# An eighth ring slot, spaced loads and a new visit order in a transformer block's down projection, with one score pipeline in its attention stage

## The chip, the cores and the metric

The kernel runs on one core of a Trainium2 chip. The metric is the device time of one execution in microseconds, taken as the median of three runs. Engines are named as in the profile: PE is TensorE, DVE is VectorE, ACT is ScalarE, POOL is GpSimd and SP is SyncE. PEclk is the clock that was granted to PE, as a share of full speed.

## The reference

One block: a normed input projection, a state-space mixer (SSD) beside a sparse attention (NSA), an output projection, and a gated feed-forward. There are 512 tokens of width 2048, the feed-forward is 5632 wide, and everything is in fp32.

```python
u = rmsnorm(h, attn_norm_w[l])
z, xbc, dt_raw, q, kc, vc, ks, vs, kw, vw, gate_raw = jnp.split(u @ w_in[l], split_at, axis=-1)
y_ssd = ssd_mixer(z, xbc, dt_raw, conv_w[l], conv_b[l], dt_bias[l], a_log[l], d_skip[l], ssd_norm_w[l])
y_att = nsa_mixer(q, kc, vc, ks, vs, kw, vw, gate_raw, cmp_w1_k[l], cmp_w2_k[l], cmp_w1_v[l], cmp_w2_v[l], cmp_pe_k[l], cmp_pe_v[l], cos, sin)
mixed = jnp.concatenate([y_ssd.astype(h.dtype), y_att.astype(h.dtype)], axis=-1)
h = h + mixed @ w_out[l]
v = rmsnorm(h, ffn_norm_w[l])
h = h + (jax.nn.silu(v @ w_gate[l]) * (v @ w_up[l])) @ w_down[l]
```

The SSD mixer's output y*silu(z) is normed over 1024 channels ahead of the output projection. The attention has 16 heads in 4 groups that share keys and values. It sums three gated branches: over keys and values compressed by a small MLP, over selected blocks (all 8 blocks of 64 tokens are selected here, so this is causal attention), and over a window of 512. A last rmsnorm closes the block.

## The kernel before, in words

**Arithmetic.** Activations lie with features on the partitions and the 512 tokens along the free axis. Every fp32 operand is split into a high part, rounded to the matmul format fp32r, and a low remainder, and every product is three matmuls: hi x hi, hi x lo, lo x hi. ACT makes the high part (`a_hi`, L118), DVE the low part (`lo`, L121), of weights too. `mul` is L124 and `add` L127.

**Order.** The program is written as coroutines. `Sched` (L67) holds tasks; `sch.tick()` after each step of a matmul group moves every task on by one, `yield n` lets n ticks pass, and `wait` holds a task until flags are set. This gives an order in which instructions are written. Outside `tc.manual_schedule()` the framework's scheduler may reorder them; inside it each engine runs them as written. Each engine works its own list strictly in order.

**Projection units.** `run_unit` (L222) computes 128 output features from 16 (w_in) or 8 (w_out) blocks of 128 weights (L241 to L243, 128x512). Weights arrive as `wraw` and become `whi` and `wlo`. The result lies in one of the PSUM banks ps_t, ps_s, ps_g, two each; a task then evacuates it and sets a flag ("evac", n) at its end, and unit n waits for the flag of unit n-2. Units run in the order `order`: dt and gates, the SSD's B, C and X, keys and values to be compressed, Z; then, for each group, values, keys and two of queries.

**Attention stage.** Before the first values unit, `pre_att` (L1010) ticks until the compressing MLP is done and swaps pools. From there on all units but the last run in `manual_schedule` (L1790). `attention` (L829) takes the groups in turn: it waits for a group's keys, values and queries, does the softmax over the compressed keys, and then sends 32 items (4 heads, 2 branches, 4 blocks of 128 rows) through 15 steps, a new item every second step: score (PE), mask and maximum (DVE, L893), exp (ACT), normalizing, transposes (PE, L926), high and low parts (`pth`, `ptl`), value matmuls (PE, L949). At a group's end the pipeline runs empty. `ev_os` (L1071) evacuates w_out's units over the SSD half of the features; the first makes the statistics of the SSD norm (`rms_stats`, "r2") and puts them into rrow. `acc2` gathers the squares of h1, the sum of x and this half. `pre_oa` drains all tasks; its `stat_s` makes the statistics of h1 (L292, L302), and OA (L1252 on, 128x512) adds the attention half of w_out.

**Gate, up and down.** These use Strassen-Winograd products: 7 products (M1 to M7) of 128x256 in place of 8, on weight quadrants 11, 12, 21, 22 and their sums S1, S3 (`quad`). `run_step` first calls `prep(s.i + 2)`, so high and low parts are made two steps ahead, in zones of R and E. For each of the 22 units u of 256 features, `g_forms` (L1457) makes the 7 forms of the gated product, high and low, in staging rows ST of the tile A (rows 44 to 72), and stores them as g_d[u], from ACT's DMA queue (L1476).

The down projection has 8 output blocks j. `VISITS` (L23) lists which j takes how many of the 22 G's at a time; sums stay in the H tiles, which `load_h` fetches. `feed` (L1541) loads a G into one of `GRING` = 7 slots, from ACT's queue, two steps after the slot's last reader (`done`). The slots lie in tiles that the gate and up projections use until their end (`start_ff`, V0, VV and T, 8 rows each, of which a G takes 7). `down_before` (L1695) loads the next H at product 1 of each visit, and opens the pool A2, rows 70 to 75 of A, for weight sums.

Of the kernel before, what the change touches and what calls it, by code (L numbers as in the profile page):

```python
# [11 lines left out]
ALU = mybir.AluOpType  # L12
# [10 lines left out]
VISITS = [(0, 3), (1, 4), (2, 5), (3, 5), (4, 5), (5, 5), (6, 5), (7, 4), (0, 4), (7, 4), (4, 5), (1, 5), (6, 5), (2, 5),  # L23
          (5, 5), (3, 6), (0, 4), (7, 4), (6, 5), (4, 6), (1, 5), (5, 6), (2, 6), (3, 5), (0, 5), (7, 4), (1, 4), (6, 4),
          (7, 6), (6, 3), (3, 6), (5, 6), (1, 4), (2, 6), (4, 6), (0, 6)]
GRING = 7
# [21 lines left out]
V_SLOT = [0, 1, 4, 5, 3, 2, 6]  # L48
# [60 lines left out]
def body(ctx, tc, xT, w_in, w_out, w_gate, w_up, w_down, w1k, w1v, cols, rows, kst, out):  # L109
# [46 lines left out]
    g_d = dram.tile([NP, 4, 128, 896], F32, name="g_d")  # L156

# [63 lines left out]

    def run_unit(u):  # L222
# [8 lines left out]
        p = p[:, 0:u.cols[1] - u.cols[0]]  # L231
        for i, k0, n in u.sub:
# [89 lines left out]
    def ev_dtg(p):  # L322
# [3 lines left out]
        mul(dve, t, p[0:64, :], rrow[0:64, :])  # L326
        yield 2
# [46 lines left out]
    def conv(t, p):  # L374
# [4 lines left out]
        mul(dve, xp[:, 3:515], p, rrow)  # L379
        y = sp.tile([128, 512], F32, tag="c", name="cv", bufs=3)  # L380
# [179 lines left out]
    def ev_z(t):  # L560
        def ev(p):
            yield from sch.wait("r1", ("y", t // 4))
            g, j = divmod(t, 4)
            if g == 0:
                sp = pools["ssd"][1]
                zs = sp.tile([128, 512], F32, tag="zs", name="zs", bufs=2)
                mul(dve, zs, p, rrow)
                act.activation(zs, zs, AF.Silu)
# [4 lines left out]
            else:  # L573
# [6 lines left out]
                mul(dve, zs, p, rrow)  # L580
                yield 1
# [16 lines left out]
    def ev_kc(g):  # L598
        def ev(p):
# [5 lines left out]
            for n, b in (("kc2", 0), ("vc2", 64)):  # L605
                for par in range(2):
                    mul(dve, R[n][par * 64:par * 64 + 64, g, :], p[b:b + 64, par::2], rrow[b:b + 64, par::2])
            if g == 3:
                sch.flags.add("kc")
# [91 lines left out]
    def ev_vs(g):  # L701
        def ev(p):
# [4 lines left out]
            mul(dve, t, p, rrow)  # L707
            yield 2
# [39 lines left out]
    def ev_ks(g):  # L748
        def ev(p):
# [4 lines left out]
            mul(dve, t, p, rrow)  # L754
            yield 1
# [32 lines left out]
    def ev_q(g, j):  # L788
        def ev(p):
# [4 lines left out]
            mul(dve, t, p, rrow)  # L794
            yield 1
# [32 lines left out]

    def attention():  # L829
        yield from sch.wait("att", "cmp")  # L830
        ap = pools["att"][1]
        vpad = ap.tile([128, 4, 128], F32R, name="vpad")
# [3 lines left out]
        for g in range(4):  # L836
            yield from sch.wait(("k", g), ("v", g), ("q", g, 0), ("q", g, 1))
            kh, kl = R["k", g]
            v = R["v", g]

            sc = R["sc", g]
            sm = ap.tile([128, 3, 4, 4], F32, tag="sm", name="sm", bufs=1)
            dve.tensor_reduce(sm[:, 0], sc, AX.X, ALU.max)
            dve.tensor_scalar(sm[:, 0], sm[:, 0], -1e20, None, op0=ALU.max)
# [1044 lines left out]
```

## Time and profile before

| What | Value |
|---|---|
| three runs | 2313.32, 2312.17, 2308.17 us |
| median | 2312.17 us |
| the profiled execution (span; the profile gives no other time for it) | 2311.7 us |
| units of w_in, attention and w_out end | at 818 us |
| OA begins | at 827 us |
| first matmul of the down projection | at 1800 us |
| PE busy | 2196.5 us, 95% |
| DVE, ACT, POOL busy | 1809.7, 1091.2, 422.2 us |
| bytes moved by DMA | 417.34 MB, mean 181 GB/s |

In the lists of waits, a row names the engine, the tile it writes and its line, then the releaser with its tile and line, and the total, the number and the longest of the waits in us. In the time lines a row has the start, the length, the engine, the line and the operation, and in brackets the idle time before it with its releaser. A window's row gives for each engine the busy time and, behind x, the number of instructions.

### The profile page before, as it was taken

To read this page: it belongs to the slowest core of one execution; us is meant where nothing else is said; L and a number is where in the kernel's file an instruction comes from. 1 tells how busy PE (TensorE), PEld (TensorE's weight loads), DVE (VectorE), ACT (ScalarE), POOL (GpSimd) and SP (SyncE) were. 2 spreads that over 40 slices of the span, in tenths; PEclk is the share of its full clock that TensorE was granted. 3 is DMA by queue.
4 is the path that set the end of the run, shared out by engine and by line. 5 is a ranking of instruction groups with operands and counts; after the bars stand their busy time and mean duration, and the time that the engine had idled before them with its cause. 6 is when DMAs were issued, how large, how long until landed. Compare 5 with 4: busy or idle time off the path is not lost. (4 is left out here: it accounts for less than half of the span.)

```text
span 2311.7 us, 39742 instructions
## 1 busy us (share of the span) xinstructions
PE 2196.5 (95%) x15376; PEld 2039.8 (88%) x15376; DVE 1809.7 (78%) x2921; ACT 1091.2 (47%) x1768; POOL 422.2 (18%) x435
## 2 busy tenths in 40 slices
PE   7999988989989989999999999999999698989997
PEld 5888877878878878999999999999999698989997
DVE  7799754768788857888888888888888697878786
ACT  4554433757676634544444444444444243333353
POOL 1011214132232134100000000000101121212122
PEclk9999989999999999999999999999999899999998
DMA  5222432221233366787878787887878857677776
GB/s 176 89 74 74 133 110 87 73 72 63 76 101 125 105 198 180 207 233 219 242 217 243 221 249 226 245 227 231 233 219 250 323 170 264 186 254 233 259 162 171
DMA packets 151469, 417.34 MB, mean 181 GB/s; under 512 B 16320, under 2 KB 21968, under 8 KB 151280
## 3 DMA queue, kind: packets, MB, share of 16 engines
q1 hardware_dynamic: 99264, 250.99, 31.5%
q0 software_dynamic: 25456, 76.78, 17.3%
q10 hardware_dynamic: 26560, 87.04, 10.5%
q8 instruction: 120, 1.97, 0.3%
q14 instruction: 69, 0.57, 0.1%
HBM read 353.67 MB, written 57.15 MB: 178 GB/s over the span
## 5 line engine op out<-in xcount | busy, mean ns | idle before, releaser
L118 ACT ACTIVATE R<-Z 128x1024 fp32r<-128x1024 f32 (+4 forms) x488 | 441.5, 922 | 573.0 <-DVE Z L127 320.6
L121 DVE TENSOR_TENSOR R<-Z,R 128x1024 fp32r<-128x1024 f32 (+4 forms) x381 | 392.3, 1035 | 28.5 <-ACT R L118 19.7
L241 PE MATMUL ps_g<-u,whi 128*128 128x512 f32 x720 | 301.1, 418 | 9.5 <-ACT whi L118 9.5
L242 PE MATMUL ps_g<-u,whi 128*128 128x512 f32 x720 | 284.3, 395 | 0.0
L243 PE MATMUL ps_g<-u,wlo 128*128 128x512 f32 x720 | 284.3, 397 | 0.0
L1252 PE MATMUL ps_g<-u,R 128*128 128x256 f32 (+1 forms) x834 | 250.5, 300 | 0.7 <-ACT R L118 0.7
L1253 PE MATMUL ps_g<-u,R 128*128 128x256 f32 (+1 forms) x834 | 249.7, 299 | 0.0
L1254 PE MATMUL ps_g<-u,R 128*128 128x256 f32 (+1 forms) x674 | 200.5, 298 | 0.1
L1252 PE MATMUL ps_t<-u,R 128*128 128x256 f32 x688 | 194.0, 282 | 0.0
L1253 PE MATMUL ps_t<-u,R 128*128 128x256 f32 x688 | 193.9, 282 | 0.0
L1252 PE MATMUL ps_s<-u,R 128*128 128x256 f32 x686 | 193.7, 282 | 0.0
L1253 PE MATMUL ps_s<-u,R 128*128 128x256 f32 x686 | 193.5, 282 | 0.0
L118 ACT ACTIVATE whi<-wraw 128x512 fp32r<-128x512 f32 x196 | 122.4, 626 | 145.2 <-PE ps_g L242 94.6
L121 DVE TENSOR_TENSOR wlo<-wraw,whi 128x512 fp32r<-128x512 f32 x196 | 145.9, 748 | 46.1 <-ACT whi L118 45.4
L241 PEld LDWEIGHTS ps_g<-u,whi 128*128 128x128 f32 x720 | 137.7, 191 | 33.1 <-ACT whi L118 11.4
L1252 PEld LDWEIGHTS ps_g<-u,R 128*128 128x128 f32 x834 | 158.3, 190 | 6.6 <-ACT R L118 0.9
L243 PEld LDWEIGHTS ps_g<-u,wlo 128*128 128x128 f32 x720 | 136.7, 190 | 30.7 <-DVE wlo L121 0.7
L1253 PEld LDWEIGHTS ps_g<-u,R 128*128 128x128 f32 x834 | 158.3, 190 | 5.9
L1254 PE MATMUL ps_s<-u,R 128*128 128x256 f32 x566 | 160.0, 283 | 0.6 <-DVE R L121 0.6
L242 PEld LDWEIGHTS ps_g<-u,whi 128*128 128x128 f32 x720 | 137.7, 191 | 19.7
L121 DVE TENSOR_TENSOR E<-Z,R 128x1024 fp32r<-128x1024 f32 x107 | 130.4, 1218 | 5.6 <-ACT R L118 5.6
L127 DVE TENSOR_TENSOR Z<-Z 128x1024 f32<-128x1024 f32 (+5 forms) x119 | 126.2, 1061 | 8.3 <-POOL Z L127 5.3
(449 smaller groups left out, 6464.3 us busy)
## 6 DMA issues: line engine op xcount, KB each, us to landing
Z<-in_w_gate SPq DMA_DIRECT2D x96, 512.0 KB, 5.3
Z<-in_w_up SPq DMA_DIRECT2D x94, 512.0 KB, 7.3
wraw<-in_w_in SPq DMA_DIRECT2D x164, 256.0 KB, 3.0
g_d<-A ACTq DMA_DIRECT2D x22, 1792.0 KB, 7.1
u<-g_d ACTq DMA_DIRECT2D x12, 1792.0 KB, 16.3
Z<-in_w_gate POOLq DMA_DIRECT2D x37, 512.0 KB, 7.4
Z<-in_w_up POOLq DMA_DIRECT2D x36, 512.0 KB, 5.6
Z<-in_w_down SPq DMA_DIRECT2D x52, 320.0 KB, 5.8
```

Of the source, the lines that this page charges most:

```text
L118: act.activation(dst, src, AF.Copy, scale=scale)
L121: eng.tensor_tensor(dst, src, f(hi), ALU.subtract)
L127: eng.tensor_tensor(o, a, b, ALU.add)
L241: pe.matmul(p, hi_t[i][:, j, :], ah, start=(k == 0), stop=False)
L242: pe.matmul(p, hi_t[i][:, j, :], al, start=False, stop=False)
L243: pe.matmul(p, lo_t[i][:, j, :], ah, start=False, stop=(k == u.nk - 1))
L1252: pe.matmul(q, h[:, k, :], ah, start=(k == 0), stop=False)
L1253: pe.matmul(q, h[:, k, :], al, start=False, stop=False)
L1254: pe.matmul(q, l[:, k, :], ah, start=False, stop=(k == s.blk.n - 1))
```

## The change

1. **PSUM released early.** Every evacuation calls `was_read(p)` behind the instruction that reads the bank, and this sets the "evac" flag; before, it was set when the whole task ended.
2. **One score pipeline.** The softmax over compressed keys becomes a task `compressed(g)` of its own. The items of all four groups go through one pipeline, an item every second step when its group's keys, values and queries are there; only the value matmuls of a group's first head wait for ("pre", g).
3. **Order of units and pools.** A group's units are now keys, queries, queries, values. `att_mem` swaps the pools as a task, and no unit waits for it. `manual_schedule` is gone from the units.
4. **Early SSD norm.** `ssd_norm` makes its statistics once all 8 tiles gy are there and puts them into acc2. The squares of h1 are gathered in rrow.
5. **Last gate and up unit by products.** Unit 21 runs both sides of each product in turn (`SEQ_L`), each into one bank. `last_out` and `last_gate` put the quadrants together; S3 is made by a DVE subtraction in place of an accumulating DMA. A slot of the ring thus comes free every two steps (`done`), starting 12 steps ahead of the end.
6. **Eighth slot, spaced loads, visits.** The eighth slot is the unused row 7 of the seven tiles. G's with u % 8 == 7 are stored in g8_d and loaded in 7 pieces of 256 KB. `feed` issues a load only when the step's planned time `clock` (0.118 us per matmul) has passed `pace`, 7 us after the load before. `VISITS` starts with two of G's per visit.
7. **Looking ahead.** In the down projection `prep` goes up to 5 us ahead, if a zone has room and the weights were asked for (`ready`).
8. **H and A2.** The H loads of visits 1 and 3 come at product 4, and A2 opens in visit 3, not in visit 1.

```diff
-VISITS = [(0, 3), (1, 4), (2, 5), (3, 5), (4, 5), (5, 5), (6, 5), (7, 4), (0, 4), (7, 4), (4, 5), (1, 5), (6, 5), (2, 5),
...
-GRING = 7
+VISITS = [(0, 2), (1, 2), (2, 3), (3, 4), (4, 5), (5, 6), (6, 6), (7, 6), (1, 6), (0, 5), (2, 6), (3, 6), (4, 6), (5, 6),
...
+GRING = 8
+G_US, MM_US, AHEAD_US = 7.0, 0.118, 5.0
...
+    def was_read(p):
+        sch.flags.add(("evac", unit_of[id(p)]))
...
-            sch.flags.add(("evac", n_u))
+            assert ("evac", n_u) in sch.flags
...
+        for g in range(4):
+            sch.add(compressed(g))
...
+        items = [(g, h, br, i) for g in range(4) for h in range(4) for br in range(2) for i in range(4)]
...
-            for t in range(2 * n + 15):
-                for d in sorted(stages, reverse=True):
-                    if (t - d) % 2 == 0 and 0 <= (t - d) // 2 < n:
-                        stages[d](*items[(t - d) // 2])
-                yield 1
-            sch.flags.add(("a", g))
+            if at < len(items) and t - last >= 2:
+                g = items[at][0]
+                if all(x in sch.flags for x in (("k", g), ("v", g), ("q", g, 0), ("q", g, 1))):
+                    live.append((items[at], t))
+                    last, at = t, at + 1
...
     def pre_att():
-        sch.run_until("cmp", *[("gy", t) for t in range(4)])
+        sch.add(att_mem())
...
+    def ssd_norm():
+        yield from sch.wait(*[("gy", t) for t in range(8)])
+        yield from hold("m")
+        yield from rms_stats(acc2, 1024, acc2, "r2")
+        held.remove("m")
...
-            if c == 0:
-                yield from hold("m")
-                yield from rms_stats(acc2, 1024, rrow, "r2")
-                held.remove("m")
...
-        prep(s.i + 2)
+        far = s.i + 2
+        while far + 1 < len(steps) and items[s.i][0].down and clock[far + 1] <= clock[s.i] + AHEAD_US:
+            far += 1
+        prep(far, s.i + 2)
...
+                forms = [P2["V0"], P2["VV"][:, 0], P2["VV"][:, 1]] + [P2["T"][i] for i in range(4)]
+                P2["slot"] = [[forms[a][:, i] for i in range(7)] for a in V_SLOT]
+                P2["slot"].append([forms[a][:, 7] for a in V_SLOT])
...
+    for slot, p in enumerate(SEQ_L):
+        bk = pair_bank()
+        for side in range(2):
+            b, sums = qs[NP - 1, side]["form"][p]
+            s = Step(b, v_rhs(p), bk(side), after=last_out(p) if side else None, sums=sums)
+        done[slot - GRING] = s.i
+    done[-1] = s.i
...
-        if n < NP and done.get(n - GRING, i) + 2 <= i:
...
+            if done.get(n - GRING, i) + 2 <= i and clock[i] >= pace["at"]:
...
+                pace["at"] = clock[i] + (G_US if a is None else G_US / 7)
+                pace["n"] += 1
...
-            if n == 1 and v:
+            if n == (4 if v in (1, 3) else 1) and v:
                 assert v < NJ - 2 or not any(fz.busy[NZ2:])
+                if v == 1:
+                    sch.run_until(("g", NP - 1))
                 load_h(v + 1)
-                P2["A2"] = P2["A"][:, 70:76, :]
+                if v == 3:
+                    P2["A2"] = P2["A"][:, 70:76, :]
...
-            with tc.manual_schedule():
-                run_unit(u)
+            run_unit(u)
```

Where the scheduler now sets the order, PE's list in the middle of the attention stage shows it. This is a piece of it before; `ps_g` rows belong to a unit, `ps_s` to scores, `ps_t` to transposes.

```order
L242 MATMUL ps_g<-u,whi 128x512
L926 MATMUL ps_t<-ident,e 128x128 x2
L241 MATMUL ps_g<-u,whi 128x512
L242 MATMUL ps_g<-u,whi 128x512
L243 MATMUL ps_g<-u,wlo 128x512
L883 MATMUL ps_s<-kh,rq 128x256
L884 MATMUL ps_s<-kl,rq 128x256
L241 MATMUL ps_g<-u,whi 128x512
L242 MATMUL ps_g<-u,whi 128x512
L243 MATMUL ps_g<-u,wlo 128x512 x2
L926 MATMUL ps_t<-ident,e 128x128 x3
```

The same stage in PE's list after the change; 20 unit matmuls stand between these rows and the burst ahead, 21 behind them (`ps_v` are the value matmuls).

```order
L251 MATMUL ps_g<-u,whi 128x512
L905 MATMUL ps_s<-kh,rq 128x384
L906 MATMUL ps_s<-kl,rq 128x384
L975 MATMUL ps_v<-pth,v 128x512
L905 MATMUL ps_s<-kh,rq 128x512
L906 MATMUL ps_s<-kl,rq 128x512
L975 MATMUL ps_v<-ptl,v 128x512
...
L975 MATMUL ps_v<-ptl,v 128x128
L948 MATMUL ps_t<-ident,e 128x128 x5
L252 MATMUL ps_g<-u,wlo 128x512
```

Item matmuls that stood one by one after three unit matmuls now stand together in bursts of about two items.

The second place is the end of the stage, where OA begins. PE's list before has the last unit of w_out, the two steps of the statistics of h1 (`ps_m`) and OA.

```order
L242 MATMUL ps_g<-u,whi 128x512
L243 MATMUL ps_g<-u,wlo 128x512
L292 MATMUL ps_m<-ones,acc_95 128x1 x4
L302 MATMUL ps_m<-ident,rst 128x128 x4
L1252 MATMUL ps_g<-u,R 128x512
```

After the change it reads as follows; the last unit matmul and the first of the two steps (L302) stand above these rows, with five transposes and eight value matmuls between L302 and them.

```order
L948 MATMUL ps_t<-ident,e 128x128 x2
L312 MATMUL ps_m<-ident,rst 128x128 x4
L948 MATMUL ps_t<-ident,e 128x128 x7
L975 MATMUL ps_v<-pth,v 128x512
L975 MATMUL ps_v<-ptl,v 128x512
L975 MATMUL ps_v<-pth,v 128x384
L975 MATMUL ps_v<-ptl,v 128x384
L975 MATMUL ps_v<-pth,v 128x256
L975 MATMUL ps_v<-ptl,v 128x256
L975 MATMUL ps_v<-pth,v 128x128
L975 MATMUL ps_v<-ptl,v 128x128
L1319 MATMUL ps_g<-u,R 128x512
```

The last items of attention moved behind the last unit of w_out, to both sides of the statistics.

The third place is DVE's list at the start of the down projection. Before, the first low parts of w_down's blocks (`R<-Z`) are 384 wide, and the last `g_forms` begins among them (L1466).

```order
L121 TENSOR_TENSOR R<-Z,R 128x384
L127 TENSOR_TENSOR Z<-Z 128x384
L121 TENSOR_TENSOR R<-Z,R 128x384
L127 TENSOR_TENSOR A<-ps_s,A 128x512
L124 TENSOR_TENSOR A<-A 128x1024
L1466 TENSOR_TENSOR A<-A 128x2x256
```

After the change they are 256 wide, with the gate products of the last unit (L126) and its last sums (`A<-ps_s`, `A<-ps_t`) among them.

```order
L123 TENSOR_TENSOR R<-Z,R 128x256
L129 TENSOR_TENSOR A<-ps_s,A 128x2x256
L126 TENSOR_TENSOR A<-A,rrow 128x2x256
L129 TENSOR_TENSOR Z<-Z 128x256
L123 TENSOR_TENSOR R<-Z,R 128x256
L129 TENSOR_TENSOR A<-ps_t,A 128x256
L123 TENSOR_TENSOR R<-Z,R 128x256 x2
L126 TENSOR_TENSOR A<-A 128x256
L129 TENSOR_TENSOR A<-ps_g,A 128x512
L123 TENSOR_TENSOR R<-Z,R 128x256
L1534 TENSOR_TENSOR A<-A 128x2x256
```

The last unit's sums, its gate and its `g_forms` (L1534) now fall into visits of two blocks instead of three.

More of the change, by code (lines that the diff above doesn't have):

```diff
@@ L919, in trans @@
-            def trans(h, br, i):
-                e, m = pr[h, br, i]
-                if i == 0:
-                    pt[h, br] = (ap.tile([128, 13, 128], F32R, tag="pth", name="pth", bufs=2),
-                                 ap.tile([128, 13, 128], F32R, tag="ptl", name="ptl", bufs=2))
-                p = ps_t()
-                for kb in range(i + 1):
-                    pe.transpose(p[:, kb * 128:(kb + 1) * 128], e[:, kb * 128:(kb + 1) * 128], ident)
-                pr[h, br, i] = p[:, 0:128 * (i + 1)].rearrange("p (a b) -> p a b", b=128)
@@ new lines, in trans @@
+        def trans(g, h, br, i):
+            e, m = pr[g, h, br, i]
+            if i == 0:
+                pt[g, h, br] = (ap.tile([128, 13, 128], F32R, tag="pth", name="pth", bufs=2),
+                             ap.tile([128, 13, 128], F32R, tag="ptl", name="ptl", bufs=2))
+            p = ps_t()
+            for kb in range(i + 1):
+                pe.transpose(p[:, kb * 128:(kb + 1) * 128], e[:, kb * 128:(kb + 1) * 128], ident)
+            pr[g, h, br, i] = p[:, 0:128 * (i + 1)].rearrange("p (a b) -> p a b", b=128)
@@ L1010, in pre_att, with att_mem @@
     def pre_att():
-        sch.run_until("cmp", *[("gy", t) for t in range(4)])
+        sch.add(att_mem())
+    def att_mem():
+        yield from sch.wait("cmp", *[("gy", t) for t in range(4)])
         close_pool("cmp")
@@ L1166, in hl_place @@
         return take(n, hz.find(n, NR, range(0, NR, 8)), ez.find(n))
-    loads, items, steps = [], [], []
+    loads, items, steps, clock = [], [], [], []
     nxt = {"raw": 0, "form": 0, "item": 0}
@@ L1203, in hl_ap, with ready, form @@
         return z.ap(at, items[i][0].n)
-    def form(upto):
+    def ready(i):
+        b, n = items[i][0], items[i][0].n
+        if hz.busy.count(False) < 14 or not hz.find(n, NR, range(0, NR - 5, 6)):
+            return False
+        advance()
+        return b.at is not None
+    def form(upto, must=None):
         while nxt["form"] <= min(upto, len(items) - 1):
             i = nxt["form"]
+            if must is not None and i > must and not ready(i):
+                return
             b, sums = items[i]
@@ L1211, in form @@
             assert b.at is not None, (i, fz.busy)
+            if b.src is None and b.both is None:
+                (x, y), = sums
+                dve.tensor_tensor(b.ap(), x.ap(), y.ap(), ALU.subtract)
+                x.read()
+                y.read()
+                sums = ()
             for x, y in sums:
@@ L1240, in __init__ @@
             steps.append(self)
+            clock.append(clock[-1] + 3 * MM_US * steps[-2].blk.n if clock else 0.0)
     def run_step(s):
@@ L1522, in body @@
     done = {}
-    for u in range(1, NP):
+    for u in range(1, NP - 1):
         for side in range(2):
```

400 lines of the change are left out of this document (250 added, 150 removed).

## The prediction

> **What bounds the kernel now.** I read the page first, then the granted clock and the busy time of each engine in stretches of 50 us, then the waits of TensorE, and last the time lines around the longest waits.
>
> ```profile
> span 2311.7 us, 39742 instructions
> PE 2196.5 (95%) x15376; PEld 2039.8 (88%) x15376; DVE 1809.7 (78%) x2921; ACT 1091.2 (47%) x1768; POOL 422.2 (18%) x435
> ```
>
> TensorE (PE) is the bound. The change leaves its matmuls as they are, so it can save only what PE idles or runs at a lowered clock. Where that is shows in a table by stretches. Its columns are the busy time of each engine, then the granted clock, the share of the DMA engines in use, and GB/s.
>
> ```profile
> core 0: us, PE busy (x) PEld busy (x) DVE busy (x) ACT busy (x) POOL busy (x), PEclk, DMA share, GB/s
> 300.00:350.00 50.00, 41.49 (x207) 33.80 (x206) 24.99 (x54) 18.42 (x42) 8.48 (x15) 0.83 0.28 95
> 350.00:400.00 50.00, 43.76 (x205) 35.59 (x204) 23.61 (x39) 20.16 (x35) 25.48 (x26) 0.97 0.27 84
> 400.00:450.00 50.00, 49.58 (x254) 41.52 (x253) 35.05 (x118) 34.18 (x87) 6.28 (x8) 0.97 0.23 76
> 500.00:550.00 50.00, 44.77 (x219) 36.96 (x218) 35.79 (x104) 29.28 (x74) 7.76 (x9) 0.93 0.21 70
> 650.00:700.00 50.00, 41.52 (x221) 34.63 (x220) 41.28 (x116) 36.40 (x87) 15.96 (x15) 0.90 0.29 97
> 800.00:850.00 50.00, 42.69 (x186) 34.82 (x186) 24.95 (x35) 16.72 (x25) 15.66 (x17) 0.93 0.54 174
> 1100.00:1150.00 50.00, 50.00 (x425) 50.00 (x424) 41.08 (x45) 22.83 (x26) 5.21 (x6) 1.00 0.83 236
> 1800.00:1850.00 50.00, 31.82 (x230) 31.22 (x229) 32.24 (x48) 15.01 (x26) 10.06 (x6) 0.80 0.80 307
> 1900.00:1950.00 50.00, 43.51 (x342) 42.90 (x341) 37.47 (x58) 17.94 (x29) 9.74 (x8) 0.93 0.79 269
> 2000.00:2050.00 50.00, 43.00 (x354) 42.79 (x353) 38.03 (x56) 16.72 (x25) 11.49 (x9) 0.95 0.87 294
> 2150.00:2200.00 50.00, 44.23 (x350) 43.51 (x348) 36.50 (x58) 17.66 (x29) 8.51 (x7) 0.93 0.75 253
> ```
>
> An undisturbed stretch of the gate and up projections (1100 to 1150) holds 425 matmuls of 128x256, or 0.118 us each. The four disturbed stretches of the down projection hold 230+342+354+350 = 1276 of the same matmuls where 4x425 = 1700 would fit: 424 are missing, and at 0.118 us that is **50 us lost**. Idle time is 18.2+6.5+7.0+5.8 = 37.5 us of it. The other 12.5 us is lost to the clock, whose shortfall is 50x(0.20+0.07+0.05+0.07) = 19.5 us; so a shortfall of 1 us costs 0.64 us, since part of it falls on idle time.
>
> The same count for the attention stage, idle time plus 0.64 of the shortfall: 8.5+5.4 = 13.9 us in 300 to 350 (the MLP that compresses keys and values ends there); 6.2+1.0 in 350 to 400, 1.0 in 400 to 450 and 5.2+2.2 in 500 to 550, together 15.6 us (ends of groups 0 and 1); 8.5+3.2 = 11.7 us in 650 to 700; 7.3+2.2 = 9.5 us in 800 to 850 (statistics ahead of OA, the half of the output projection that takes attention's rows). Together **50.7 us lost**.
>
> The waits of PE over the whole span name what released them (line waited for: us in total, times, longest):
>
> ```profile
> PE ps_t L1254 <- DVE R L121: 12.0, 3, 11.2
> PE ps_g L241 <- ACT whi L118: 9.5, 6, 3.2
> PE ps_t L1252 <- DMA V<-g_d: 7.0, 1, 7.0
> PE ps_t L1252 <- DMA T<-g_d: 6.9, 1, 6.9
> PE ps_g L1252 <- DMA T<-g_d: 6.0, 1, 6.0
> PE ps_g L1252 <- DMA V<-g_d: 4.8, 1, 4.8
> PE ps_m L292 <- DVE acc L127: 4.7, 1, 4.7
> PE ps_t L926 <- DVE ptl L121: 4.4, 4, 2.6
> PE ps_t L864 <- DVE sc L124: 3.9, 2, 2.0
> PE ps_m L302 <- POOL rst L298: 2.3, 1, 2.3
> ```
>
> **The down projection.** Four of these waits, 7.0+6.9+6.0+4.8 = 24.7 us, are for tensors G read back from g_d. Their loads take, in the list of DMA issues (size, median us to landing):
>
> ```profile
> g_d<-A ACTq DMA_DIRECT2D x22, 1792.0 KB, 7.1
> u<-g_d ACTq DMA_DIRECT2D x12, 1792.0 KB, 16.3
> T<-g_d ACTq DMA_DIRECT2D x6, 1792.0 KB, 13.9
> Z<-in_w_down SPq DMA_DIRECT2D x40, 256.0 KB, 4.5
> ```
>
> A load is issued when its ring slot was read for the last time. With 7 slots and the old visits some G are wanted less than 14 to 16 us after that. The new visits and the eighth slot widen it: counted by the steps of the new order at 0.118 us per matmul, the tightest case has 12.4 us, for a 256 KB piece (4.5 us by the nearest row), and every whole G has 22.7 us or more. All 24.7 us should go. What is late next is the weight stream, which has no row among the waits of PE; no cost.
>
> The longest wait, 11.2 us, only looks like VectorE's. Time lines of ACT's issues, of POOL and of DVE show its cause (start, length, what, and in brackets the idle time before and its releaser):
>
> ```profile
> 1812.36 1.07 ACTq L1476 DMA_DIRECT2D g_d<-A  x1
> ...
> 1835.67 1.53 POOL L127 TENSOR_TENSOR A<-Z 128x640 f32<-128x640 f32 x1 [31.10 <-DMA g_d<-A]
> ...
> 1838.84 0.82 DVE L127 TENSOR_TENSOR E<-E,A 128x640 f32<-128x640 f32 x1 [12.64 <-POOL Z L127]
> ```
>
> The last G is stored from rows of A which the pool A2 takes over in visit 1. POOL's sum into A2 waits until the store, issued at 1812, has landed; DVE waits for POOL, and PE for DVE. The change opens A2 in visit 3, two visits later, so the 11.2 us goes. With the waits gone the clock should stay up: 12.5 us more. Removed: 24.7+11.2+12.5 = 48 us, which with the small waits makes the 50 us of the table.
>
> It is not all kept. The first two visits now have two blocks each, 2x2x7x3 = 84 matmuls or 9.9 us. In DVE's new order I count, from the sum that ends the last unit's products to the end of visit 1, 24 instructions of 256 columns, 9 of 512 and one of 1024. Their prices are in the groups by shape between 1850 and 2280 us:
>
> ```profile
> L127 DVE TENSOR_TENSOR A<-ps_g,A 128x256 f32<-128x256 f32 x11 | 4.6, 415 | 0.4 <-ACT A L1589 0.4
> L127 DVE TENSOR_TENSOR A<-ps_g,A 128x512 f32<-128x512 f32 x34 | 23.4, 688 | 16.6 <-PE ps_g L1254 16.2
> ```
>
> 24x0.415 + 9x0.688 + 1.4 = 17.6 us, the last term an estimate, twice that of 512. DVE thus falls 7.7 us behind PE at most, less by the lead it has, and half clock follows: 2.3 us at 0.3 us per us of wait, the ratio of 12.5 to 37.5. I put **10 us** on this (bounds 0, if the lead holds, and 30, if the loads are late too: see the rivals). Down: 50-10 = **40 us** gained.
>
> The last gate and up unit, done product by product: the same 42 matmuls per side and 11 fewer DVE instructions in all, beside work that PE hides (1100 to 1150 has DVE at 41 of 50 us). I cost it at nothing; without that cover 11x0.69 = 8 us either way. What matters is that the slots of G come free one by one ahead of the end, and the loads start earlier.
>
> **The attention stage.** Four things change at once.
>
> Early release of PSUM (the evac flag set behind the read) and scheduler order remove the `whi` waits, 9.5 us, whose cause is that the manual order leaves a unit's weights behind other ACT work. One pipeline over all groups removes the drain at the end of groups 0, 1 and 2 and with it the `sc` waits, 3.9 us: the 15.6 and the 11.7 us above. The compressing MLP now has unit matmuls between its own; I leave it 3 of its 13.9 us (bounds 0 and 13.9), for its last chain.
>
> What appears instead: in PE's new order two stretches near the fifth unit of w_out, of some nine and five items, have no unit matmul between them, since units ran ahead. The nearest row is the `ptl` wait, 4 times for 4.4 us: **5 us** (bounds 0 and 14x1.1 = 15).
>
> The SSD norm, done early, should take its statistics off the end, but the end is not gone. Here it is before:
>
> ```profile
> 817.45 0.39 PE L242 MATMUL ps_g<-u,whi 128*128 128x512 f32 x1
> 817.68 0.39 PE L243 MATMUL ps_g<-u,wlo 128*128 128x512 f32 x1
> 822.81 1.46 PE L292 MATMUL ps_m<-ones,acc 128*128 128x1 f32 x8 [4.74 <-DVE acc L127]
> 826.56 1.11 PE L302 MATMUL ps_m<-ident,rst 128*128 128x128 f32 x4 [2.29 <-POOL rst L298]
> 827.33 0.78 PE L1252 MATMUL ps_g<-u,R 128*128 128x512 f32 x1
> ```
>
> These are the statistics of h1, not those of the SSD norm, and they still come after the last w_out unit. PE works in order, and the new order places the last 10 items' transposes and value matmuls around and behind these two steps, with ACT's hi parts for OA (the R instructions) behind the last item's pth. So the same 4.7 and 2.3 us stand in a row with one more wait, at most a `ptl` of 2.6, and a half clock of 3.4: **13 us** (bounds 7 and 20) where 9.5 stood. Attention: 50.7-3-5-13 = **30 us** gained.
>
> [...]
>
> **The sum.** 2311.7-40-30 = 2241.7 us on the profiled execution, whose span lies 0.5 us below the median of the runs (2312.17): **2242 us**, 3.0% faster. About 0.2% (5 us) is what a measurement can tell from no change.
>
> **The rivals.**
>
> *The start of the down projection is bound by transfers* (0.17). Before, it already was, around the same place (us, clock, DMA share, GB/s):
>
> ```profile
> 1802.00:1808.00 6.00, 0.58 1.03 402
> 1820.00:1826.00 6.00, 1.00 1.03 403
> ```
>
> Between 30 us ahead of the first matmul and 40 us behind it the new order moves two stores and eight loads of G (10x1.84 = 18.4 MB), 3 or 4 H loads (2 MB), the last unit's weights (4 MB) and about 4 MB of w_down: 28 MB. At 403 GB/s this takes 70 us, exactly the time there is. If it does not fit, or if the H load queued behind g_d's last store on ACT's queue comes late, the start loses 30 instead of 10 us: 2262 us. For: the DMA share of 1.03. Against: the first visits need only two or three G.
>
> [...]
>
> *Nearly all stalls vanish* (0.17): DVE's lead covers the two short visits, and the drain at the end of attention hides the statistics of h1. Then 2311.7-50-51 = 2211 us. For: PE has some 8 us of item matmuls to put there. Against: they wait for the same DVE and ACT.
>
> *The attention stage gains nothing* (0.09): its waits move to the end, where no units are left to cover the items. 2311.7-40 = 2272 us. For: units run ahead of items in the new order. Against: DVE has 25 of 50 us free in 300 to 400, which the single pipeline can use.
>
> *Slower, by the bursts in attention* (0.05, and 0.02 that it comes out even). In the manual order a score, a transpose or a value matmul comes after every third unit matmul. In the scheduler's, the 128 items (4 groups, 4 heads, 2 branches, 4 blocks of rows) come about two at a time, 64 bursts, with some 20 unit matmuls between two. PE works in order, so a burst that is not ready stops the units behind it. 70 us of gain over 64 bursts decide at 1.1 us per burst, which is what the `ptl` wait shows on average (4.4 in 4). At the 1.6 us of the `whi` waits (9.5 in 6) 64 bursts cost 102 us: 2344 us. For: ACT and DVE share PSUM buffers with the bursts. Against: some 20 unit matmuls between two bursts, begun 0.23 us apart in the time line above, are 4.6 us of cover.
>
> **How the numbers follow.** The forecast has 0.50 at 2242, the transfers 0.17 at 2262, no stalls 0.17 at 2211, no gain in attention 0.09 at 2272, bursts 0.05 at 2344, even 0.02. Faster: 0.93, same 0.02, slower 0.05. The range holds the forecast and the first three rivals with the bounds that go with them: 2209 below, 2 us under the case without stalls; above, the 2272 of the third rival and 6 of the 7 us by which the end of attention may exceed its term, 2278. The bursts and the even case lie outside.
>
> **What would show it.** Right: no wait on g_d above 1 us; no wait of DVE for POOL near the store of the last G; a clock of 1.00 in the windows of the down projection but its first; 10 us of idle or half clock in that first one, with DVE as releaser; no `sc` wait; 13 us between the last w_out matmul and OA beyond its matmuls. Wrong: waits on g_d left or moved to weights; in attention many waits of 1 us or more at transposes; a start of the down projection with DMA share 1 and PE waiting for a DMA.

## The result, and the profile after

The changed kernel takes 2255.9 us (median of four runs, 2252.0 to 2259.1), against 2311.3 us for the kernel before beside it: a ratio of 0.9759, interval 0.9742 to 0.9776. That is 55 us faster. The forecast was 2242 us, in a range of 2209 to 2278: the direction and the stages were right, the saving was 55 us where 70 were forecast. One of the four runs of e5 (below) took 5526.8 us and is left out of its median. The two profiled executions give 2311.7 and 2253.6 us of span, and their time lines show where the 58 us between them come from (us; the stages end with the start of the next):

| Stage | before | after | change | forecast |
|---|---|---|---|---|
| up to the first unit of the attention stage | 334.2 | 314.1 | -20.1 | |
| from there to the first matmul of OA | 493.1 | 474.6 | -18.5 | |
| both together | 827.3 | 788.7 | **-38.6** | -30 |
| OA, gate and up projections but the last unit | 932.5 | 933.1 | +0.6 | 0 |
| last gate and up unit | 39.8 | 41.3 | +1.5 | 0 |
| down projection | 494.6 | 473.1 | **-21.5** | -40 |
| behind it | 17.4 | 17.5 | +0.1 | 0 |

So the attention stage gave more than forecast, and the down projection about half. (The first two rows are not like for like: a group's first unit is now its keys, and it runs between matmuls of the compressing MLP.) The windows that answer to those of before (busy time and instructions of PE, PEld, DVE, ACT, POOL, then granted clock, DMA share, GB/s) show both:

```profile
300.00:350.00 50.00, 48.34 (x277) 41.17 (x276) 31.71 (x65) 26.54 (x57) 23.27 (x32) 1.00 0.40 126
350.00:400.00 50.00, 50.00 (x255) 42.42 (x254) 37.18 (x91) 34.53 (x71) 14.81 (x12) 1.00 0.29 95
500.00:550.00 50.00, 50.00 (x279) 43.23 (x278) 42.24 (x112) 35.12 (x85) 17.93 (x19) 1.00 0.21 68
600.00:650.00 50.00, 47.52 (x239) 39.87 (x238) 45.35 (x116) 37.10 (x87) 13.63 (x12) 0.93 0.44 141
650.00:700.00 50.00, 46.63 (x230) 37.69 (x229) 43.87 (x117) 35.19 (x88) 15.64 (x15) 0.93 0.31 99
750.00:800.00 50.00, 43.42 (x204) 35.42 (x203) 29.36 (x68) 23.44 (x50) 9.38 (x11) 0.90 0.38 129
1900.00:1950.00 50.00, 48.23 (x398) 47.01 (x397) 34.97 (x48) 17.56 (x23) 7.97 (x6) 1.00 0.83 273
2000.00:2050.00 50.00, 49.80 (x420) 49.52 (x420) 38.78 (x54) 19.41 (x26) 8.15 (x6) 1.00 0.82 258
2150.00:2200.00 50.00, 48.29 (x396) 47.00 (x395) 44.78 (x75) 25.88 (x45) 16.38 (x16) 1.00 0.75 180
```

In the attention stage PE is busy throughout in 350 to 400 and 500 to 550, and loses time in 600 to 700 and at the end. In the down projection's middle the clock stays at 1.00. The waits of PE over the whole span no longer name g_d, `whi` or the transposes of `sc`; their place in the down projection is taken by many short waits for DVE's low parts (R). `em` and `ptl` are those of the attention items, and the wait of L1319 is the start of OA:

```profile
PE ps_s L1321 <- DVE R L123: 7.6, 13, 2.0
PE ps_g L1321 <- DVE R L123: 6.7, 9, 1.6
PE ps_t L1321 <- DVE R L123: 5.6, 10, 0.8
PE ps_s L905 <- DVE em L915: 3.8, 4, 2.0
PE ps_g L1319 <- ACT R L120: 3.7, 2, 3.5
PE ps_t L948 <- DVE ptl L123: 0.6, 2, 0.3
```

Cut into its first four visits, the middle and the last four, the down projection reads (PE busy, clock, DMA share, GB/s):

```profile
1763.05:2236.11 473.06, 452.84 (x3708) 0.99 0.75 227
1763.05:1807.03 43.98, 34.41 (x234) 0.88 0.85 314
1807.03:2188.80 381.77, 378.32 (x3173) 1.00 0.76 231
2188.80:2236.11 47.31, 40.11 (x306) 1.00 0.55 116
```

At 0.118 us a matmul, the whole would take 436 us for its 3696 weight matmuls; 37 us are still lost, where the same stage of before (494.6 us) lost 58.6. The losses by visit, each visit's time less 21 matmuls for each block, are 16.8 us in the first four (2, 2, 3 and 4 blocks), 7.6 in the middle and 12.6 in the last four (3, 3, 3 and 5 blocks).

### The profile page after: what moved, and what is told of

Read it like the earlier page. It is cut to its first block, busy times and chain, and to the rows that moved or that the text cites. A ratio compares the mean times of both kernels' runs of the same rounds, so it can differ in the third digit from the quotient of the medians.

```text
span 2253.6 us, 39735 instructions
## 1 busy us (share of the span) xinstructions
PE 2183.8 (97%) x15376; PEld 2034.1 (90%) x15376; DVE 1812.0 (80%) x2910; ACT 1092.2 (48%) x1765; POOL 426.9 (19%) x432
## 3 DMA queue, kind: packets, MB, share of 16 engines
q0 software_dynamic: 24816, 75.28, 17.5%
q10 hardware_dynamic: 28288, 87.04, 11.1%
## 4 chain that ended last, share of the span: by engine, by line
PE 54%; DVE 4%; DMA 3%; issue 1%; ACT 1%; POOL 1%; ACTq 0%; DVEq 0%; SPq 0%; POOLq 0%
PE ps_g L1321 7%; PE ps_g L1319 7%; PE ps_g L1320 7%; PE ps_t L1321 6%; PE ps_t L1319 6%; PE ps_t L1320 6%; PE ps_s L1321 5%; PE ps_s L1319 5%; PE ps_s L1320 5%; DVE R L123 2%; DMA Z<-in_w_down 1%; DMA E<-in_w_down 1%; DVE A L129 1%; DMA A<-h_d 1%; DVE Z L129 1%
## 5 line engine op out<-in xcount | busy, mean ns | idle before, releaser
L120 ACT ACTIVATE R<-Z 128x1024 fp32r<-128x1024 f32 (+4 forms) x479 | 435.9, 927 | 556.1 <-DVE Z L129 315.3
L123 DVE TENSOR_TENSOR R<-Z,R 128x1024 fp32r<-128x1024 f32 (+5 forms) x373 | 389.0, 1048 | 29.5 <-ACT R L120 21.3
L250 PE MATMUL ps_g<-u,whi 128*128 128x512 f32 x720 | 287.5, 399 | 0.3 <-DVE h L126 0.3
L251 PE MATMUL ps_g<-u,whi 128*128 128x512 f32 x720 | 283.7, 394 | 0.0
L1319 PE MATMUL ps_g<-u,R 128*128 128x256 f32 (+1 forms) x844 | 252.8, 300 | 3.7 <-ACT R L120 3.7
L123 DVE TENSOR_TENSOR wlo<-wraw,whi 128x512 fp32r<-128x512 f32 x196 | 151.3, 775 | 59.4 <-ACT whi L120 58.2
L1319 PE MATMUL ps_s<-u,R 128*128 128x256 f32 x699 | 196.3, 281 | 0.0
L1320 PE MATMUL ps_s<-u,R 128*128 128x256 f32 x699 | 195.9, 280 | 0.0
L1319 PE MATMUL ps_t<-u,R 128*128 128x256 f32 x673 | 189.7, 282 | 0.2 <-ACT R L120 0.2
L1320 PE MATMUL ps_t<-u,R 128*128 128x256 f32 x673 | 189.3, 281 | 0.0
L1319 PEld LDWEIGHTS ps_g<-u,R 128*128 128x128 f32 x844 | 159.2, 189 | 9.6 <-ACT R L120 4.0
L1320 PEld LDWEIGHTS ps_g<-u,R 128*128 128x128 f32 x844 | 159.6, 189 | 5.9
L1321 PE MATMUL ps_s<-u,R 128*128 128x256 f32 x571 | 160.9, 282 | 2.2 <-DVE R L123 2.1
L1321 PEld LDWEIGHTS ps_g<-u,R 128*128 128x128 f32 x676 | 127.7, 189 | 8.8 <-DVE R L123 4.7
```

The lines of the kernel that those rows point to most:

```text
L120: act.activation(dst, src, AF.Copy, scale=scale)
L123: eng.tensor_tensor(dst, src, f(hi), ALU.subtract)
L250: pe.matmul(p, hi_t[i][:, j, :], ah, start=(k == 0), stop=False)
L251: pe.matmul(p, hi_t[i][:, j, :], al, start=False, stop=False)
L1319: pe.matmul(q, h[:, k, :], ah, start=(k == 0), stop=False)
L1320: pe.matmul(q, h[:, k, :], al, start=False, stop=False)
```

## The experiments

Each saving is against the kernel before on the same chip in the same comparison; the changed kernel saves 55.3 us on this scale. L numbers of variants of the changed kernel are its own.

| Run | median us | saves us | ratio to before (interval) |
|---|---|---|---|
| e1 attention alone | 2276.7 | 34.1 | 0.9854 (0.9834 to 0.9874) |
| e2 down alone | 2289.9 | 21.0 | 0.9911 (0.9896 to 0.9926) |
| e5 scheduler's order alone | 2293.7 | 17.5 | 0.9919 (0.9902 to 0.9935) |
| e3 changed, manual order | 2303.6 | 7.2 | 0.9965 (0.9951 to 0.9979) |
| e10 changed, late flag | 2257.1 | 56.1 | 0.9763 (0.9746 to 0.9780) |
| e8 changed, denser items | 2275.1 | 36.1 | 0.9848 (0.9831 to 0.9866) |
| e4 changed, longer visits | 2261.7 | 49.1 | 0.9791 (0.9775 to 0.9807) |
| e7 changed, H2 first | 2256.2 | 55.0 | 0.9767 (0.9751 to 0.9784) |
| e6 changed, sums left out | 2252.6 | 58.5 | 0.9741 (0.9725 to 0.9757) |
| e12 changed, e6 and e7 | 2252.1 | 61.0 | 0.9741 (0.9723 to 0.9758) |
| e11 changed, A2 in visit 1 | 2258.6 | 54.6 | 0.9766 (0.9744 to 0.9787) |
| e9 changed, other end visits | 2252.3 | 60.8 | 0.9737 (0.9720 to 0.9754) |

### The two halves

e1 is the kernel before with the diff's parts 1 to 4, e2 with parts 5 to 8; neither has an edit of its own.

> The kernel before with parts 1 to 4 of the change alone (early release of PSUM, one score pipeline, unit order without the manual schedule, early SSD norm); the down projection is the old one. My theory: the two halves of the change lie in different stages and add up, so this saves the 38.6 us that the traces show up to the start of OA: 2273 us, within 4. Rival: the stages touch each other (the state that the attention stage leaves for OA and the gate projection), and the time is off by more than 5 us from that.

> The kernel before with parts 5 to 8 alone (last unit by products, eighth slot, spaced loads, visits, looking ahead, H and A2). My theory: it saves the 21.5 us of the down projection less the 1.5 us of the last unit: 2292 us, within 4. Rival: the down projection saves the forecast 40 us when the attention stage is the old one, 2272 us.

34.1 and 21.0 us add up to 55.1, the whole change. e2 gives what the traces had shown for its stages (20 us), e1 4.5 us less than they had (38.6). The halves are independent, and the down projection does not give 40 us with the old attention stage either. In e1 the old stall is back in the old visits: POOL waits for the store of the last G.

```profile
1799.05 1.53 POOL L127 TENSOR_TENSOR A<-Z 128x640 f32<-128x640 f32 x1 [31.67 <-DMA g_d<-A]
```

### The attention stage

e3 takes the changed kernel and puts the manual schedule back:

```diff
-            run_unit(u)
+            with tc.manual_schedule():
+                run_unit(u)
```

> The changed kernel with the units of the attention stage back in the manual schedule. My theory: written order puts a unit's weights behind other work of ACT, so the whi waits of before (9.5 us) come back and with them some half clock: 10 to 15 us slower than the changed kernel, about 2268 us. Rival (bursts): the scheduler's bursts cost PE waits, and without them the time falls by up to 10 us, to 2246.

It is 48 us slower than the changed kernel, three to five times what I expected. The rival, that bursts cost more than they bring, falls. The `whi` waits did come back, but they are only 7.9 us of it. The windows of e3 show where it hurts: the compressing MLP ends with nothing beside it, as before, and later stretches idle too.

```profile
300.00:350.00 50.00, 40.99 (x190) 32.86 (x190) 25.23 (x55) 18.22 (x41) 10.01 (x18) 0.76 0.28 91
350.00:400.00 50.00, 44.17 (x203) 35.73 (x202) 27.67 (x54) 22.16 (x45) 21.18 (x20) 0.93 0.21 67
...
450.00:500.00 50.00, 43.23 (x215) 35.56 (x213) 27.60 (x58) 22.95 (x50) 18.01 (x19) 0.93 0.19 60
```

e5 does the reverse: the kernel before, with only `manual_schedule` taken away.

> The kernel before with one edit: the manual schedule is taken away from the units of the attention stage; code, pipeline by groups and evac flags stay the old ones. Putting the manual schedule back into the changed kernel cost 47 us, more than the whole attention stage had gained (e3_manual), so the written order of the new code is worse than that of the old. Theory A (the scheduler's order does nearly all): this alone saves 25 us or more, 2285 or less. Theory B (the single pipeline and the early flags give the scheduler its room): in the old code units still wait for the evac flag at the end of a task and the pipeline still drains at each group's end, so it saves under 12 us, 2299 or more.

17.5 us lie between the two theories: the order alone gives half of the 34, and the new code adds the other half. In e5 OA waits 6.9 us at its start, and the attention stage ends 35 us after the last unit (units end at 765.5, OA begins at 800.8; 19.0 us in the changed kernel):

```profile
PE ps_g L1252 <- ACT R L118: 6.9, 1, 6.9
```

Old code drains its pipeline at every group's end, and with the units running ahead in the scheduler's order that drain falls where no unit is left. e3 and e5 together say that neither the new code nor the order does all of it alone: the new code in manual order loses 14 us in this stage (7.2 us saved, of which the down projection has 21.0; in the trace OA begins at 838.1, 10.8 us later than before), the order in the old code saves 17.5, both together 34.

e10 sets the evac flag at the task's end again.

```diff
     def was_read(p):
-        sch.flags.add(("evac", unit_of[id(p)]))
+        pass
...
-            assert ("evac", n_u) in sch.flags
+            sch.flags.add(("evac", n_u))
```

> The changed kernel with the evac flag set at the end of the evacuation task again, as before; scheduler's order, single pipeline and early norm stay. The scheduler's order alone saved 17 us and all parts of the attention stage 34, so 17 us are left for pipeline, flags and norm. If the early flag carries most of it, this is 8 us slower or more: 2264 at least. If it is the single pipeline, the flag matters little here: 2256 to 2260.

56.1 us against 55.3: the early release makes no difference that can be seen, and the other half belongs, in the scheduler's order, to the pipeline, the order of units and the early norm together. They were not taken apart further.

e8 starts every fourth item earlier.

```diff
-            if at < len(items) and t - last >= 2:
+            if at < len(items) and t - last >= (1 if at % 4 == 3 else 2):
```

> The changed kernel with every fourth item of the score pipeline started one step after the one ahead instead of two, so that the pipeline ends 32 steps earlier, under w_out's units. The drain between the last unit and OA, 19.0 us in the changed kernel, has 7.7 us of item matmuls. If it is the late items that hold OA up, it falls to the 9.5 us that the statistics took before, and the time to about 2249. If the extra density costs waits in the stage (bursts), the stage loses as much ahead of the last unit, and the time stays at 2256, within 3, or rises.

Half of each theory came true. The drain fell from 19.0 to 10.0 us (units end at 798.0, OA begins at 808.0), but the last unit ends 28 us later (a part of that is item matmuls that moved ahead of it), and the kernel is 19 us slower than the changed one. Its windows:

```profile
600.00:650.00 50.00, 43.17 (x225) 35.65 (x224) 43.46 (x115) 36.56 (x87) 15.61 (x17) 0.93 0.31 101
650.00:700.00 50.00, 43.82 (x205) 35.63 (x204) 35.32 (x111) 29.43 (x78) 4.97 (x5) 0.83 0.17 59
700.00:750.00 50.00, 45.41 (x228) 37.20 (x226) 45.69 (x125) 35.42 (x91) 19.64 (x19) 0.97 0.43 135
```

Between 600 and 800 PE waits 16.7 us for tiles of the items (`em`, `ptl`, `pth`, `at`). This is the burst rival's mechanism, at another density: bursts that come closer than their exponentials, maxima and low parts are ready stop the units behind them. At the spacing of the change it costs 10 us (600 to 700 above).

### The down projection

e4 changes `VISITS`: none of 2 blocks, two of 3 at the start, none below 4 later, a last one of 6.

```diff
-VISITS = [(0, 2), (1, 2), (2, 3), (3, 4), (4, 5), (5, 6), (6, 6), (7, 6), (1, 6), (0, 5), (2, 6), (3, 6), (4, 6), (5, 6),
+VISITS = [(0, 3), (1, 3), (2, 4), (3, 6), (4, 5), (5, 6), (6, 6), (7, 6), (1, 5), (0, 5), (2, 5), (6, 5), (4, 6), (3, 5),
...
-          (5, 5), (4, 5), (6, 4), (0, 3), (1, 3), (2, 3), (7, 5)]
+          (3, 6), (5, 6), (0, 4), (2, 4), (6, 6), (4, 6), (7, 6)]
```

> The changed kernel with other visits: two of 3 blocks and none of 2, where the changed kernel has two of 2 and four of 3, and the last of 6 instead of 5. My theory: visits of 2 and 3 blocks are bound by DVE, whose sums out of PSUM cost the same for each visit whatever its length. Counted by what each length lost in the changed kernel (5 us for 2 blocks, 2.4 for 3, 0.5 for 4, 3 for a short last visit) the loss falls from 24.6 to 9 us: 2241 us, within 5. Rival (transfers): the start is bound by loads, G 2 has only 14 us of slack instead of 24, waits on g_d come back, and the time is 2256 us or more.

It saves 6 us less than the changed kernel. The end did as the theory said (6.0 us lost in the last five visits). The start did not: its first three visits lost 3.8, 5.5 and 9.1 us, and the last of these is one arrival. DVE waits for H2, whose load stands behind the last G's store on ACT's queue, and PE waits for DVE (time lines of DVE and of PE):

```profile
1798.54 0.42 DVE L129 TENSOR_TENSOR A<-ps_s,A 128x256 f32<-128x256 f32 x1 [6.53 <-DMA A<-h_d]
```

```profile
1799.62 0.58 PE L1321 MATMUL ps_g<-V,R 128*128 128x256 f32 x1 [5.86 <-DVE R L123]
```

My theory of short visits fell for the start, in this form. The next three runs ask what limits it. e7 issues H2's load ahead of the store:

```diff
+        if u == NP - 1:
+            load_h(2)
         if u % GRING == GRING - 1:
...
-                if v == 1:
-                    sch.run_until(("g", NP - 1))
-                load_h(v + 1)
+                if v > 1:
+                    load_h(v + 1)
```

e6 leaves DVE work out:

```diff
-                d_add(j, pr, p, first, last)
+                if not (first and j < 4 and pr in (M6, M7, M5)):
+                    d_add(j, pr, p, first, last)
```

> The changed kernel with the load of H2 issued ahead of the store of the last G on ACT's queue, as soon as the staging rows that it takes were read, instead of behind that store. In e4_longer_visits DVE waited 6.5 us for this load, in the changed kernel 1.0 and 2.1 us for H loads. If these arrivals hold up the start, its 2.1 us go, with the half clock behind it 3 to 4 us: 2252. If DVE's own work is the limit, the waits only move: 2256, within 2.

> The changed kernel, which leaves out part of the computation: DVE's sums out of PSUM of the products M6, M7 and M5 in the first visits of blocks 0 to 3, about 2.9 us of DVE work per visit at 0.69 us for 512 and 0.42 for 256 columns. If the start of the down projection is bound by DVE's work in short visits, the 16.8 us that the first four visits lose fall to about 6, and the time to 2246. If it is bound by arrivals (the H load of visit 2, transfers at 402 GB/s), the loss stays above 13 and the time above 2252.

> The changed kernel with both e6 (DVE's sums of M6, M7 and M5 left out in the first visits of blocks 0 to 3) and e7 (H2's load ahead of the last store). Alone they cut the loss of the first four visits from 16.8 to 10.1 and to 14.5 us. If DVE's work and the arrival of H2 are two limits of which each hides the other, both together bring it to 6 us or less, and the time to 2246. If a third limit holds, transfers or POOL, it stays near 10.

In the changed kernel DVE waited 3.1 us for H tiles at the start:

```profile
DVE A L129 <- DMA A<-h_d: 3.1, 2, 2.1
```

e7 has no such wait, and its time is the same (2256.2): the loss of the first four visits went from 16.8 to 14.5 us, and 1.1 came back in the fifth. Without the sums (e6) they lose 10.1 us, in an execution that is e6's fastest and 6 us under its median; by time e6 saves 3 us more than the changed kernel. With both (e12) they lose 10.5, not the 6 that I expected; by time e12 saves 4 to 6 us more. Both intervals overlap with that of the changed kernel. So in the traces DVE's sums are worth some 6 us there and H2's arrival hardly any. What is left in e12 has two parts. Visit 3 waits once for the next H:

```profile
DVE A L129 <- DMA A<-h_d: 5.1, 1, 5.1
```

And visits 0 and 1 still lose 6.7 us, with DVE (third busy time) at work for most of them:

```profile
1766.80:1775.00 8.20, 5.72 (x44) 5.11 (x43) 6.70 (x15) 3.46 (x10) 2.01 (x2) 1.00 1.03 399
1775.00:1783.40 8.40, 5.92 (x45) 5.29 (x45) 8.16 (x15) 3.91 (x9) 2.87 (x2) 1.00 0.73 253
```

DVE's and POOL's time lines of e12 show where its work is stretched:

```profile
1778.74 3.92 DVE L123 TENSOR_TENSOR R<-Z,R 128x256 fp32r<-128x256 f32 x5
```

```profile
1778.10 1.51 POOL L129 TENSOR_TENSOR Z<-Z 128x512 f32<-128x512 f32 x1 [6.83 <-DMA Z<-in_w_down]
1779.69 1.35 POOL L129 TENSOR_TENSOR Z<-Z,E 128x512 f32<-128x512 f32 x1
```

Five low parts of 256 columns took 3.92 us, where one alone takes 0.42; POOL's sums ran beside them. The last section comes back to this.

e11 opens A2 in visit 1 again.

```diff
-                if v == 3:
+                if v == 1:
                     P2["A2"] = P2["A"][:, 70:76, :]
```

> The changed kernel with the pool A2 opened in visit 1 again, on rows that the last G's store still reads. The store is issued at 1778 us, in visit 1. If my reading of the old 11.2 us wait is right, a sum or a load into A2 waits for the store again and PE with it: 4 to 11 us slower, 2260 to 2267. If the new visits need no block in A2 so early, or the old wait had another cause: 2256, within 2.

54.6 us against 55.3: no difference. The wait for the store is there all the same. A weight load into the pool waits for it on SP's queue (ACT's time line, then SP's waits and time line), and no wait of PE above 1.2 us follows:

```profile
1777.62 0.38 ACTq L1547 DMA_DIRECT2D g_d<-A  x1
```

```profile
SPq L1240 <- DMA g_d<-A: 6.6, 1, 6.6
1785.29 0.33 SPq L1240 DMA_DIRECT2D A<-in_w_down  x1
```

Two things differ from the old stall. The store holds A2 up for 7.7 us from its issue, where the kernel before had it from 1812.36 to 1835.67, 23 us, with three loads of G issued in the 14 us ahead of it (one in e11). And the first to want A2 is a load with time to spare, not a sum of POOL that DVE and PE wait for. So opening the pool later is not what removed the 11.2 us. The new visits, the spaced loads or both did; no run separates them. (e1 and e5, with the old down projection, have the stall back.)

e9 leaves the start and changes the end alone: in place of (7, 5), (0, 6), (1, 5), (2, 5) and the last (0, 3), (1, 3), (2, 3), (7, 5):

```diff
+          (6, 6), (7, 6), (0, 6), (1, 6), (2, 5), (3, 6), (4, 6), (6, 6), (5, 5), (7, 4), (0, 5), (1, 4), (2, 4), (3, 6),
+          (5, 5), (4, 5), (6, 4), (0, 4), (1, 4), (2, 4), (7, 6)]
```

> The changed kernel with its start of the down projection left alone and only the end of the visits changed: three visits of 3 blocks become 4, the last one 6 instead of 5. In e4_longer_visits the last five visits lost 6 us where the changed kernel's last four lose 12.6. If visits of 3 blocks are bound by DVE, whose sums cost the same for any length, this saves 5 to 7 us: 2250. If what e4 saved there was an accident of its other visits, the time stays at 2256, within 2.

It saves 60.8 us, 5.5 more than the changed kernel against their own controls and 3.6 by medians, but the intervals overlap; the traced down projection is 2 us shorter. Here are two visits of 3 blocks in the changed kernel, and two of 4 in e9:

```profile
2198.50:2208.50 10.00, 8.42 (x65) 7.62 (x64) 8.50 (x18) 5.51 (x11) 1.72 (x2) 1.00 0.71 169
2208.50:2218.60 10.10, 8.23 (x65) 7.66 (x65) 9.29 (x17) 5.94 (x11) 3.93 (x4) 1.00 0.52 111
```

```profile
2180.40:2191.50 11.10, 10.48 (x86) 10.06 (x85) 10.12 (x18) 6.26 (x11) 3.94 (x4) 1.00 0.82 188
2191.50:2202.60 11.10, 10.21 (x86) 10.01 (x85) 10.80 (x18) 6.37 (x11) 3.36 (x4) 1.00 0.65 159
```

A visit of 3 has 63 matmuls of its own, 7.4 us, and takes 10.1 with DVE busy for 8.5 to 9.3. One of 4 takes 11.1 for 9.9 us of matmuls, with 1.6 us more of DVE time: 2.6 us lost each against 1.2. DVE is not alone in it: in each visit of 3 it waits 0.7 to 1.3 us for a high part that ACT makes. The last visit lost 5 us with 6 blocks as with 5, so its length was not the cause; with 6 blocks it lost 2.6 in e4 and 2.1 in the kernel before. e9 is the fastest complete kernel of this study, by a margin that these runs do not settle.

## Why the prediction was right, and where its sizes were off

**G loads (24.7 us): right.** No wait on g_d is left, as the slack of the new order said. What the spacing of the loads, the eighth slot or the visits bring alone was not tried.

**The A2 wait (11.2 us): right in size, not in what removes it.** It went, and e1 and e5 keep it with the old down projection. But e11 shows that opening A2 two visits later was not needed: with the rest of the change the store that took 23 us takes 8, and the first load into A2 can wait for it.

**The clock (12.5 us): mostly right.** It is 1.00 in the windows that had 0.93 to 0.95. The first four visits keep 0.88 (see the last section).

**The start of the down projection (10 us forecast, 16.8 measured): right for the visits that it priced, and two visits short.** The term was made for the two visits of 2 blocks. They lost 4.1 and 6.1 us, 10.2 together, and DVE was busy for 7.74+9.85 = 17.6 us in them, as priced. Such a close hit is in part luck: 1.7 us of it are instructions that stretched beside POOL (last section), which no price had. What failed is where the count ended: the next two visits, of 3 and 4 blocks, lost another 6.6 us for which the sum has no term. That DVE's sums cost some 6 of the 16.8 us is shown by e6 and e12; the rest is read from PE's waits for R, not tested. The rival of transfers (2262) did not come: the loss is not 30 us, no wait of PE names a load, and in e7 the arrivals that DVE waited for in visits 0 and 2 are gone while the time stayed, although the DMA share of these visits is 0.85.

**What the sum did not have.** I compared only the four worst windows and took the rest as unchanged. Of the 58.6 us that the old down projection lost I counted 50 as gone and 10 as new, which leaves 18.6. It is 37: the start is 6.8 over its term, and the middle and the last four visits lose 7.6+12.6 where 8.6 was left. The new visits end with 3, 3, 3 and 5 blocks, the old with 4, 6, 6 and 6, and the old four lost only some 4 us. The price of DVE's work in short visits I had applied to the start alone.

**The last unit by products (nothing): nearly right,** 1.5 us slower.

**The attention stage (30 us forecast, 38.6 measured): right in direction, its size only in part explained.** I left 3 us for the compressing MLP, and 300 to 350 idles 1.7 at full clock. I counted no gain in the windows that were not quoted: PE idled 1.3 us in 450 to 500 and 1.5 in 550 to 600, 4 in all of them, and now idles nowhere between 350 and 600. The two stretches without unit matmuls cost 10 us instead of 5: 2.5+3.4 us idle in 600 to 700 and 0.64x7 for the clock. With the end these bring the 30 to about 32; the other 6 to 7 us have no term. The end came near its 13 us by luck, for the waits that I put there did not come. Its time line shows both steps of the statistics (L302, L312) among the last items without a wait, and ACT's hi parts late for OA:

```profile
769.27 0.39 PE L252 MATMUL ps_g<-u,wlo 128*128 128x512 f32 x1
...
773.79 0.50 PE L967 MATMUL ps_v<-cph,vpad 128*128 128x512 f32 x1 [1.54 <-DVE at L129]
...
774.39 1.16 PE L302 MATMUL ps_m<-ones,rrow 128*128 128x1 f32 x8
...
780.33 1.06 PE L312 MATMUL ps_m<-ident,rst 128*128 128x128 f32 x4
...
788.69 0.68 PE L1319 MATMUL ps_g<-u,R 128*128 128x512 f32 x1 [3.50 <-ACT R L120]
```

It takes 19.0 us from the last unit to OA, some 8 of them item matmuls: 11 us where 13 were forecast. I had put the 4.7 and 2.3 us waits of the statistics there again. The items hide them, as the rival of vanishing stalls had it; in their place PE waits 1.5 us for `at`, 1.4 for `pth` and `ptl` and 3.5 for ACT's hi parts, and the clock is 0.90 in 750 to 800. No run shows the 3.4 us of half clock that I had added there, an estimate of mine; in steps of 1 us the clock is 0.50 from 776 to 782. I ascribed the gain to early release and scheduler order with the pipeline as one. e10 shows that the release counts for nothing that can be seen, e5 that the order alone gives half, and e3 that the rest of the new code gives the other half only in that order.

**The slower rival** (bursts, 0.05) did not come, but e8 shows that its mechanism is real and near: a quarter of the items one step earlier, and the kernel is 19 us slower.

## What to carry to other kernels

Count what a new order costs in the stretches that were good, not only what it saves in the bad ones: here an order of visits that removed 36 us of waits gained 21, mostly because its short visits at both ends no longer covered the work of another engine. Parts of a change that look like the cause (early release, the later pool) can be worth nothing once another part is in; only undoing them one at a time tells.

## What the runs showed of the hardware

In the first four visits of the changed kernel, instructions of DVE that read two tensors from SBUF took longer while POOL summed. POOL ran two sums from 1797.35 to 1800.88 (one row, x2):

```profile
1797.35 3.53 POOL L129 TENSOR_TENSOR Z<-Z 128x640 f32<-128x640 f32 x2 [20.43 <-DMA Z<-in_w_down]
```

```profile
1797.40 2.05 DVE L123 TENSOR_TENSOR R<-E,R 128x512 fp32r<-128x512 f32 x1
1799.37 0.41 DVE L129 TENSOR_TENSOR A<-ps_t,A 128x256 f32<-128x256 f32 x1
1799.70 1.72 DVE L123 TENSOR_TENSOR R<-E,R 128x512 fp32r<-128x512 f32 x1
1801.35 0.68 DVE L123 TENSOR_TENSOR R<-Z,R 128x512 fp32r<-128x512 f32 x1
```

The same low part of 512 columns takes 2.05 and 1.72 us beside the sums and 0.68 behind them; the instruction between them, which reads one of its inputs from PSUM, takes its usual 0.41. The two low parts are thus 1.37 and 1.04 us longer; by what means was not shown. My sum had no term for it. Over the first four visits of the changed kernel the stretched instructions took about 4 us more than unstretched ones, 2.4 of it these two: some 1.7 in visits 0 and 1, none in visit 2, where POOL is idle. That is a small part of the 16.8 us lost, and how much of it reached PE was not measured; no run has these sums on another engine.

The clock fell without a long wait. In the first three visits of the changed kernel it was 0.81 to 0.85, though the longest wait of PE there was 2.0 us:

```profile
1763.00:1772.10 9.10, 7.22 (x45) 6.66 (x45) 7.74 (x17) 3.46 (x10) 2.01 (x2) 0.81 1.03 398
1772.10:1783.10 11.00, 7.32 (x44) 6.52 (x43) 9.85 (x19) 4.02 (x9) 2.61 (x2) 0.84 0.50 181
1783.10:1794.70 11.60, 9.38 (x65) 8.96 (x64) 7.75 (x16) 3.82 (x8) 0.00 (x0) 0.85 1.02 389
```

In steps of 1 us the clock there is 0.50 from 1769 to 1771, from 1779 to 1782 and from 1789 to 1792 us, and 1.00 for most of the time between. In the kernel before, in steps of 2 us, it is 0.50 from 1804 to 1812 us, around a wait of 6.9 us that ends at 1807, and from 1834 to 1842, around the wait of 11.2 us that ends at 1840. This is what my forecast calls half clock.

In e12 a wait of 2.9 us left it at 1.00 (window, then PE's time line):

```profile
1790.80:1804.50 13.70, 10.52 (x87) 10.11 (x86) 8.20 (x12) 5.05 (x9) 3.48 (x2) 1.00 1.03 402
```

```profile
1798.39 0.38 PE L1321 MATMUL ps_s<-V,R 128*128 128x256 f32 x1 [2.90 <-DVE R L123]
```

So in these runs the length of one wait does not decide: 2.9 us left the clock at 1.00, and waits of 2.0 us at most went with 0.81 to 0.85. The sum of short waits does not decide either: in the first two visits of e12 (above) PE waits 4.9 us in all, 1.6 at most, and the clock is 1.00; in those of the changed kernel it waits some 5.5 us in all, 2.0 at most, and the clock is 0.81 and 0.84. What decides stays open.
